# Low parts of later weights made in one buffer on GpSimd's queue, with an accumulating DMA

## The chip, the cores and the metric

The kernel runs on one core of one Trainium2 chip. The core has a matrix engine (TensorE, "PE" in the profile; "PEld" is its weight load), a vector engine (VectorE, "DVE"), a scalar engine (ScalarE, "ACT"), GpSimd ("POOL") and a queue engine that issues DMAs (SyncE, "SP"). ACT and POOL can issue DMAs too, in the order of their own queues. Each engine takes its instructions strictly in order: one that has to wait holds what stands behind it. The metric is the device time of one execution in microseconds, the median of several runs.

## What is computed

One decoder block over 1024 positions of width 1024, all in float32. A normed and modulated input `h` goes through one wide projection; two branches use its parts (stick-breaking attention, and a pooling over windows), gates mix them, and one more projection goes back to the residual stream:

```python
h = rms_norm(x, norm_gain) * (1.0 + scale) + shift
q, k, v, z_a, u, z_b, m_a, m_b = jnp.split(h @ w_in, offs, axis=-1)
p_a = (stick_breaking_attention(q, k, v) * silu(z_a)) @ w_branch_a
p_b = (multiscale_causal_pool(u, pool_w, pool_scale) * silu(z_b)) @ w_branch_b
merged = sigmoid(m_a) * p_a + sigmoid(m_b) * p_b
out = rms_norm(x + gate * (merged @ w_out), final_gain)
```

## The kernel before

The matrix engine is fed with `fp32r`, a rounded float32. To keep the accuracy of float32, each operand is split into a high part (the value, rounded to `fp32r`) and a low part (the value less its high part), and a product is made of three: high by high, high by low, low by high (`mm3`). So every weight tile of 128 x 1024 needs its low part somewhere.

The program runs through these stages, named by the tiles that the profile shows:

- `wm`, `ua`, `u`: the pooling maps are folded into weights, `h` is made, and the branch `u` is projected (its second half of the sequence, eight column tiles, in the loop that follows `load_wv` in the pool `vp`).
- `v`: the values, two halves of eight blocks each. Each block's result is split and stored to `v_d`.
- `wzb`: eight projections for the pooling branch's gate (`project(CZB + j, ...)`). Each loads its weights (`wzb_raw`), splits them on ACT and DVE, and its `silu` puts the result into `gb`. In the same loop, SP loads `w_gate` (`wg`), and DVE reduces it to the block's output gate.
- `p1` to `p7`: the product with `w_branch_b`, in seven half-size products of sums and differences (a Strassen scheme). Each has two halves; `a_op` splits the weights' side and `b_op` the other, on ACT and DVE. `load_a` (line 653) loads the weights' blocks on SP. For `p5`, each half needs three loads and adds them up on DVE.
- `p` in the attention stage: 40 projections with tiles `w` (queries, keys, gates), threaded by hand between the attention's own matmuls. Then `pa` and `o`, the two output projections.

The last 40 weight tiles are in the list `tiles`. The first eight (`PLAIN`) are split when they are loaded: high part on ACT, low part on GpSimd (`load_parts`, `split`, line 123) but for one on DVE. For the other 32, the low part is made ahead, during the `u`, `v`, `wzb` and `p1` to `p7` stages, and stored to the DRAM tensor `wl_d`; the attention stage loads it from there, beside the weights. `make_lo` (lines 147 to 165) does this: SP loads a tile into `lraw` (three buffers), ACT rounds it into `lhi` (one buffer), DVE subtracts in place, and SP stores the result. The tuples `LO_V`, `LO_ZB` and `LO_PB` say how many tiles are begun at each step of a stage: 8 in the `u` loop and 10 with `v` (in the pool `vp`), then 4 with `wzb` and 10 with the products (in the pool `pb`). `lraw` in `pb` also serves `wg` and, once, `gjunk`.

GpSimd's other work stands at both ends: small powers for the norm (line 260), and from the attention stage on the splits of the first weight tiles (line 123), the clearing of `kl` (line 790), two masks for each block of logits (`affine_select`, line 936) and a product at the end of each unit.

The order of each queue is made by the framework's planner from a simulation of the program, except for operations that `order` or `keep_in_program_order` pins: those of the first stage, and in the attention stage the matmuls and a few others. A pool's memory is used again by the pool opened after it is closed, and a tile there waits for the tiles whose place it takes. So the planner sets the place of `make_lo`'s steps in each queue, and the chip's waits then decide when they run.

Of the kernel before, what the change touches and what calls it, by code (L numbers as in the profile page):

```python
# [9 lines left out]
F32 = mybir.dt.float32  # L10
F32R = mybir.dt.float32r
AF = mybir.ActivationFunctionType
ALU = mybir.AluOpType
PSUM = bass.MemoryType.PSUM

P = 128
D = 1024
# [20 lines left out]

MASKED = 4
LO_V = (1, 0, 1, 1, 0, 1, 1, 0)  # L40
LO_ZB = (0, 1, 0, 1, 0, 1, 0, 1)
LO_PB = (1, 2, 1, 2, 1, 2, 1)

DIFFS = {1: 0, 4: 1, 7: 2, 10: 3}
HD = 64
# [12 lines left out]
def block_kernel(ctx, tc, a, out):  # L58
    nc = tc.nc
    v, act, gp = nc.vector, nc.scalar, nc.gpsimd  # L60

    def pool(name, **kw):
        return tc.tile_pool(name=name, bufs=1, reuse_waits="tile", **kw)
# [14 lines left out]
    def any_bank(name):  # L78
        return bank(next(turns), name)
# [8 lines left out]
    wl_d = dram.tile([5 * KB, P, D], F32, name="wl_d")  # L88
# [30 lines left out]
    def split(src, shape, pl, tag, bufs, hi_eng, lo_eng, name):  # L119
        hl = pl.tile([shape[0], 2] + list(shape[1:]), F32R, tag=tag, bufs=bufs, name=name)  # L120
        hi, lo = hl[:, 0], hl[:, 1]
        copy_to(hi_eng, hi, src)
        lo_eng.tensor_tensor(lo, src, hi.bitcast(F32), op=ALU.subtract)  # L123
        return hi, lo
# [15 lines left out]
    tiles = []  # L140
# [3 lines left out]
    tiles += gates  # L144
    early_lo = iter(range(PLAIN, len(tiles)))

    def make_lo(pl, n, bufs=3, later=False):

        rest = []
        for _ in range(n):  # L150
            i = next(early_lo)
            raw = pl.tile([P, D], F32, tag="lraw", bufs=bufs, name=f"l{i}_raw")
            hi = pl.tile([P, D], F32R, tag="lhi", bufs=1, name=f"l{i}_hi")
            nc.sync.dma_start(raw, a["w_in"][tiles[i]])

            def low(i=i, raw=raw, hi=hi):
                act.copy(hi, raw)  # L157
                v.tensor_sub(raw.bitcast(F32R), raw, hi.bitcast(F32))  # L158
                nc.sync.dma_start(wl_d[i], raw)

            if later:
                rest.append(low)
            else:
                low()
        return rest

    def load_parts(i, name):
        if i < PLAIN:
# [8 lines left out]
    def mm3(ps, whl, mhl, kbs, mov, first=True, last=True):  # L177
        (wh, wl), (mh, ml) = whl, mhl
        n = len(kbs)
        for i, kb in enumerate(kbs):  # L180
            for j, (w, m) in enumerate(((wh, mh), (wh, ml), (wl, mh))):
                mm(
                    ps, w[:, kb], mov(m, kb),
                    start=first and i == 0 and j == 0, stop=last and i == n - 1 and j == 2,
                )
# [4 lines left out]
    def hmov(sh):  # L190
        return lambda m, kb: m[:, kb, sh * 512:sh * 512 + 512]
# [25 lines left out]
    with pool("init") as init:  # L217
# [101 lines left out]
        wg, maps, halves = {}, {}, {}  # L319
# [66 lines left out]
        hi, lo_ = (0,), (1,)  # L386
        some, rest = slice(0, P), slice(P, D)
# [72 lines left out]
        for kb in range(KB):  # L460
            todo = [(i, kb) for i in range(len(accs))]
# [120 lines left out]
    with pool("vp") as vp:  # L582
        def load_wv(hf, k2):
            raw = wts.tile([P, 2, 512], F32, tag="raw", bufs=2, name=f"wv{hf}_{k2}_raw")
            nc.sync.dma_start(raw.rearrange("p k c -> p (k c)"), a["w_v"][hf, k2])
            return split(raw, [P, 2, 512], vp, "wv", 6, act, v, f"wv{hf}_{k2}")

        wv = [[load_wv(0, k2) for k2 in range(4)]]
        for i in reversed(range(KB)):
            ps = any_bank(f"u{i}_1")  # L590
            mm3(ps, whl[i], h, range(KB), hmov(1))
            use[i](1, ps)
            make_lo(vp, 1)
        early.close()
        diffs = ExitStack()
        todo = []
        dif = diffs.enter_context(pool("dif", side="right"))
        vouts = ExitStack()
        vop = vouts.enter_context(pool("vop", side="right"))
        for hf in range(2):  # L600
            if hf == 0:
                wv.append([load_wv(1, k2) for k2 in range(4)])
            for sb in range(8):
                ss = slice(sb * P, (sb + 1) * P)
                ps = any_bank(f"v{sb}_{hf}")
                for kb in range(KB):
                    hh, hl = h_hi[:, kb, ss], h_lo[:, kb, ss]
                    wh, wl = (w[:, kb % 2] for w in wv[hf][kb // 2])
                    for n, (l, w) in enumerate(((hh, wh), (hh, wl), (hl, wh))):
                        mm(ps, l, w, start=kb == 0 and n == 0, stop=kb == KB - 1 and n == 2)  # L610

                vo = vop.tile([P, 8, 2, HD], F32R, tag="vo", bufs=3, name=f"vo{sb}_{hf}")
                pv = ps.rearrange("p (h d) -> p h d", d=HD)
                act.copy(vo[:, :, 0], pv)
                v.tensor_sub(vo[:, :, 1], pv, vo[:, :, 0].bitcast(F32))
                nc.sync.dma_start(
                    v_d[4 * hf:4 * hf + 4, :, sb].rearrange("n p c -> p n c"),
                    vo.rearrange("p (n h) i d -> p n (h i d)", h=2).bitcast(F32),
                )

                now, todo = todo, make_lo(vp, LO_V[sb], later=True)
                if 8 * hf + sb in DIFFS:
                    j = DIFFS[8 * hf + sb]
                    todo.append(lambda j=j, u=load_u(j): make_d(j, u))
                for f in now:
                    f()
        assert not todo
        vouts.close()
# [3 lines left out]
    pb = pbs.enter_context(pool("pb"))  # L632
# [29 lines left out]
    for j in range(KB):  # L662
        if j not in dhls:
            make_d(j, load_u(j))

        def silu(sh, ps):
            z = gb[:, j, sh * 512:sh * 512 + 512]
            act.activation(z, ps, AF.Sigmoid)
            v.tensor_mul(z, ps, z)
            v.scalar_tensor_tensor(z, dhls[j][:, sh * 512:sh * 512 + 512], psc_v[:, j:j + 1], z, ALU.mult, ALU.mult)  # L670

        project(CZB + j, f"wzb{j}", silu, act, v)
        if j < 4:
            v.tensor_sub(t1[:, j], gb[:, j, 512:], gb[:, j, :512])
        else:
            v.tensor_sub(t2[:, j - 4], gb[:, j, 512:], t1[:, j - 4])
            v.tensor_sub(gb[:, j - 4, 512:], gb[:, j, 512:], gb[:, j - 4, 512:])
        make_lo(pb, LO_ZB[j])
        if j == 0:
            nc.sync.dma_start(sg, a["c_row"].broadcast_to([P, D]))  # L680
            gjunk = pb.tile([P, D], F32, tag="lraw", bufs=3, name="gjunk")
            act.activation(gjunk, sg, AF.Sigmoid)
            v.tensor_mul(sg, sg, gjunk)
        wg = pb.tile([P, D], F32, tag="lraw", bufs=3, name=f"wg{j}")
        nc.sync.dma_start(wg, a["w_gate"][j])
        v.scalar_tensor_tensor(wg, wg, 1.0, sg, ALU.mult, ALU.mult, accum_out=gate[:, j:j + 1])
        del dhls[j]
# [62 lines left out]
    for n, (name, a_of, b_of) in enumerate(products):  # L750
        c = {"p5": "b", "p3": "b", "p2": "c"}.get(name, "a")
        if c not in chain:
            chain[c] = [bank((tb if c == "b" else ta)[j], f"{name}_{j}") for j in range(4)]
        ps = chain[c]
        for q in range(2):
            wl_, ml_ = a_op(a_of(q), f"{name}a{q}"), b_op(b_of(q), f"{name}b{q}")
            for j in range(4):
                for e in range(2):
                    for i, (w, m) in enumerate(((0, 0), (0, 1), (1, 0))):
                        mm(  # L760
                            ps[j], wl_[:, w, e, j * P:(j + 1) * P], ml_[:, m, e],
                            start=name in ("p1", "p5", "p2") and (q, e, i) == (0, 0, 0), stop=(q, e, i) == (1, 1, 2),
                                skip_group_check=True,
                        )
        for j in range(4):
            if name == "p1":
                keep["s1", j] = copied("s1", 4, j, ps[j])
            elif name == "p6":
                keep["s2", j] = copied("s2", 4, j, ps[j])
            elif name == "p7":  # L770
                out_b(j + 4, 1, added(copied("s3", 2, j, ps[j]), chain["b"][j]))
            elif name == "p4":
                out_b(j + 4, 0, copied("s4", 2, j, ps[j]))
            elif name == "p3":
                out_b(j, 1, added(keep["s2", j], ps[j]))
            elif name == "p2":
                out_b(j, 0, added(keep["s1", j], ps[j]))
        make_lo(pb, LO_PB[n])
    pbs.close()


# [295 lines left out]
    with pool("fin") as fin:  # L1077
# [14 lines left out]
        for sh in range(2):  # L1092
            sl = slice(sh * 512, sh * 512 + 512)
            ms = []
            for j in range(KB):
# [9 lines left out]
                n = 0  # L1105
# [12 lines left out]
            for i in range(4):  # L1118
                sb = 4 * sh + i
# [7 lines left out]
                for c_, cl in enumerate(pieces):  # L1127
                    w_ = cl.stop - cl.start
                    ps = bank(("z", "tr")[c_ % 2], f"o{sb}_{c_}")[:, :w_]
                    n = 0  # L1130
# [85 lines left out]
```

## Time and profile before

| | |
|---|---|
| median of three runs | 1215.5 us (1214.86 to 1216.26) |
| the profiled execution | 1219.61 us, of which the span is 1217.9 us |
| mean granted clock of TensorE | 0.995 of full speed |

The profile is of one execution. Its page gives the busy time of each engine, the span in 40 slices with a digit of busy share for each, the groups of instructions by line, and the DMA queues. In rows of the order of time, the first two numbers are the start and the duration in us, then come engine, line, operation, output and inputs, the shape and the count; what stands in brackets is the idle time of the engine before it and what ended that. Rows of waits give the total in us, how often, and the longest. Rows of windows give the length and then for each engine the busy time, with the number of instructions.

### The profile page before, as it was taken

To read this page: it belongs to the slowest core of one execution; us is meant where nothing else is said; L and a number is where in the kernel's file an instruction comes from. 1 tells how busy PE (TensorE), PEld (TensorE's weight loads), DVE (VectorE), ACT (ScalarE), POOL (GpSimd) and SP (SyncE) were. 2 spreads that over 40 slices of the span, in tenths; PEclk is the share of its full clock that TensorE was granted. 3 is DMA by queue.
4 is the path that set the end of the run, shared out by engine and by line. 5 is a ranking of instruction groups with operands and counts; after the bars stand their busy time and mean duration, and the time that the engine had idled before them with its cause. 6 is when DMAs were issued, how large, how long until landed. Compare 5 with 4: busy or idle time off the path is not lost.

```text
span 1217.9 us, 16134 instructions
## 1 busy us (share of the span) xinstructions
PE 1194.0 (98%) x5698; PEld 995.8 (82%) x5698; DVE 796.7 (65%) x1088; ACT 549.9 (45%) x1020; POOL 167.9 (14%) x352
## 2 busy tenths in 40 slices
PE   8999999999699999999999999999999999999997
PEld 7888888887488888888888888888888888888886
DVE  5754591686675186777768678687777753795643
ACT  5564331332453255655656555555655653232211
POOL 1000000000000333222222221222221210000001
PEclk9999999999899999999999999999999999999999
DMA  9649994767735732343534325353353335985622
GB/s 350 259 168 360 308 380 169 231 221 166 271 138 178 224 92 70 107 135 104 162 116 138 101 95 164 110 155 99 110 143 100 96 123 173 352 273 168 208 72 84
DMA packets 85699, 212.39 MB, mean 174 GB/s; under 512 B 10609, under 2 KB 24049, under 8 KB 83442
## 3 DMA queue, kind: packets, MB, share of 16 engines
q1 hardware_dynamic: 77410, 196.47, 49.8%
q10 hardware_dynamic: 8208, 14.88, 3.3%
q8 instruction: 45, 0.74, 0.3%
q14 instruction: 36, 0.29, 0.1%
HBM read 144.20 MB, written 50.34 MB: 160 GB/s over the span
## 4 chain that ended last, share of the span: by engine, by line
PE 82%; DMA 7%; DVE 5%; issue 4%; ACT 1%; POOL 0%; SPq 0%; POOLq 0%; ACTq 0%; DVEq 0%
PE p L108 38%; PE v L108 7%; PE o L108 6%; PE z L108 6%; PE av L108 5%; PE wt L108 5%; PE pa L108 5%; PE u L108 4%; DMA wl_d<-l_raw 3%; PE ua L108 3%; DMA l_raw<-in_w_in 1%; PE wm L108 1%; DMA m<-sb_d 1%; PE wzb L108 1%; DMA kh<-kh 1%
## 5 line engine op out<-in xcount | busy, mean ns | idle before, releaser
L108 PE MATMUL p<-hT,w 128*128 128x512 f32 x1920 | 480.1, 391 | 0.6 <-ACT m_sg L203 0.6
L108 PEld LDWEIGHTS p<-hT,w 128*128 128x128 f32 x1920 | 355.2, 188 | 74.8 <-ACT m_sg L203 1.0
L938 DVE TENSOR_TENSOR_SCAN om<-om 128x512 f32<-128x512 f32 (+7 forms) x128 | 175.7, 1373 | 124.7 <-ACT om L931 69.1
L931 ACT ACTIVATE om<-z 128x512 f32<-128x512 f32 (+2 forms) x192 | 94.5, 492 | 156.4 <-PE z L108 133.9
L957 ACT CAST wt<-wt 128x512 fp32r<-128x512 f32 (+1 forms) x160 | 88.2, 551 | 48.2 <-PE wt L108 47.9
L958 DVE TENSOR_TENSOR wt<-wt,wt 128x512 fp32r<-128x512 f32 (+1 forms) x160 | 99.2, 620 | 16.2 <-ACT wt L957 15.6
L108 PE MATMUL av<-wt,vv 128*128 128x512 f32 x320 | 106.4, 414 | 0.0
L936 POOL TENSOR_SCALAR_AFFINE_SELECT om<-om 128x128 f32<-128x128 f32 x128 | 56.4, 441 | 346.9 <-ACT om L931 287.5
L108 DVE TENSOR_TENSOR be<-be,om 128x511 f32<-128x511 f32 (+7 forms) x128 | 95.1, 748 | 1.1 <-POOL be L936 0.7
L932 ACT ACTIVATE be<-z 128x512 f32<-128x512 f32 (+2 forms) x192 | 94.1, 490 | 0.0
L108 PE MATMUL pa<-ga,wa 128*128 128x512 f32 x384 | 89.9, 390 | 0.7 <-DVE s L1110 0.6
L108 PE MATMUL o<-wo,mhl 128*128 128x512 f32 (+1 forms) x408 | 89.6, 377 | 0.0
L108 PE MATMUL wzb<-hT,wzb 128*128 128x512 f32 x384 | 87.6, 390 | 2.0 <-DVE wzb L123 2.0
L108 PE MATMUL wt<-ident,be 128*128 128x128 f32 x576 | 89.4, 273 | 0.0
L108 PE MATMUL v<-wv,hT 128*128 128x512 f32 x384 | 87.2, 389 | 0.0
L108 PEld LDWEIGHTS wzb<-hT,wzb 128*128 128x128 f32 x384 | 71.9, 188 | 17.5 <-DVE wzb L123 2.5
L108 PEld LDWEIGHTS pa<-ga,wa 128*128 128x128 f32 x384 | 71.9, 188 | 16.4 <-issue 1.0
L108 PEld LDWEIGHTS o<-wo,mhl 128*128 128x128 f32 x408 | 73.5, 188 | 14.1
L108 PEld LDWEIGHTS v<-wv,hT 128*128 128x128 f32 x384 | 72.1, 188 | 14.9
L108 PEld LDWEIGHTS wt<-ident,be 128*128 128x128 f32 x576 | 70.2, 141 | 11.6
L157 ACT CAST l_hi<-l_raw 128x1024 fp32r<-128x1024 f32 x32 | 33.6, 1051 | 72.6 <-DMA l_raw<-in_w_in 54.8
L158 DVE TENSOR_TENSOR l_raw<-l_raw,l_hi 128x1024 fp32r<-128x1024 f32 x32 | 39.1, 1222 | 41.7 <-ACT l_hi L157 41.6
(175 smaller groups left out, 1481.8 us busy)
## 6 DMA issues: line engine op xcount, KB each, us to landing
w_raw<-in_w_in SPq DMA_DIRECT2D x40, 512.0 KB, 4.6
l_raw<-in_w_in SPq DMA_DIRECT2D x32, 512.0 KB, 4.9
wl_d<-l_raw SPq DMA_DIRECT2D x32, 512.0 KB, 5.9
w<-wl_d SPq DMA_DIRECT2D x32, 512.0 KB, 4.0
v_d<-vo SPq DMA_DIRECT2D x16, 512.0 KB, 5.2
vv<-v_d SPq DMA_DIRECT2D x8, 1024.0 KB, 5.3
wa_raw<-in_w_branch_a SPq DMA_DIRECT2D x16, 512.0 KB, 4.8
wa<-in_w_mod SPq DMA_DIRECT2D x7, 1024.0 KB, 6.3
```

What stands on the lines that cost most here:

```text
L108: ins = op(*args, **kw)
L157: act.copy(hi, raw)
L158: v.tensor_sub(raw.bitcast(F32R), raw, hi.bitcast(F32))
L931: act.activation(om[:, b0:b0 + n], zp[:, :n], AF.Sigmoid, scale=-0.125)
L932: act.activation(be[:, b0:b0 + n], zp[:, :n], AF.Sigmoid, scale=0.125)
L936: gp.affine_select(out=tl[:, :P], in_=tl[:, :P], pattern=[[1, P]], compare_op=ALU.is_gt, fill=fill, base=0, channel_multiplier=-1)
L938: v.tensor_tensor_scan(om[:, :W], om[:, :W], om[:, :W], 1.0, ALU.mult, ALU.min)
L957: act.copy(wt[:, 0, :off], pt[:, :off])
L958: v.tensor_sub(wt[:, 1, :off], pt[:, :off], wt[:, 0, :off].bitcast(F32))
```

## The change

`make_lo` no longer uses SP, ACT and DVE. GpSimd's queue loads the tile into one buffer `lo`; GpSimd reads it and writes the negative of its value, rounded to `fp32r`, over it; a DMA of the same queue loads the tile from DRAM again and adds it to what the buffer holds, which leaves the value less its high part; and that queue stores it to `wl_d`. The buffer `lhi` is gone, the `later` form too, so in the `v` loop the steps are no longer written behind the next block. `lraw` has four buffers in `vp` and three in `pb`. `wg` and `gjunk` get one buffer of their own. Two more tiles are begun with `wzb` and two fewer with the products: 8, 10, 6 and 8.

```diff
-LO_ZB = (0, 1, 0, 1, 0, 1, 0, 1)
-LO_PB = (1, 2, 1, 2, 1, 2, 1)
+LO_ZB = (0, 1, 1, 1, 0, 1, 1, 1)
+LO_PB = (1, 1, 1, 1, 1, 2, 1)
...
-    def make_lo(pl, n, bufs=3, later=False):
-
-        rest = []
+    def make_lo(pl, n, bufs=4):
+
         for _ in range(n):
             i = next(early_lo)
-            raw = pl.tile([P, D], F32, tag="lraw", bufs=bufs, name=f"l{i}_raw")
-            hi = pl.tile([P, D], F32R, tag="lhi", bufs=1, name=f"l{i}_hi")
-            nc.sync.dma_start(raw, a["w_in"][tiles[i]])
-
-            def low(i=i, raw=raw, hi=hi):
-                act.copy(hi, raw)
-                v.tensor_sub(raw.bitcast(F32R), raw, hi.bitcast(F32))
-                nc.sync.dma_start(wl_d[i], raw)
-
-            if later:
-                rest.append(low)
-            else:
-                low()
-        return rest
+            src = a["w_in"][tiles[i]]
+            lo = pl.tile([P, D], F32, tag="lraw", bufs=bufs, name=f"l{i}_raw")
+            gp.dma_start(lo, src)
+            gp.tensor_scalar(lo.bitcast(F32R), lo, -1.0, 0.0, op0=ALU.mult, op1=ALU.add)
+            gp.dma_start(lo, src, accum_op=ALU.add)
+            gp.dma_start(wl_d[i], lo)
...
-                now, todo = todo, make_lo(vp, LO_V[sb], later=True)
+                now, todo = todo, []
+                make_lo(vp, LO_V[sb])
...
-        make_lo(pb, LO_ZB[j])
+        make_lo(pb, LO_ZB[j], 3)
...
-            gjunk = pb.tile([P, D], F32, tag="lraw", bufs=3, name="gjunk")
+            gjunk = pb.tile([P, D], F32, tag="wg", bufs=1, name="gjunk")
...
-        wg = pb.tile([P, D], F32, tag="lraw", bufs=3, name=f"wg{j}")
+        wg = pb.tile([P, D], F32, tag="wg", bufs=1, name=f"wg{j}")
...
-        make_lo(pb, LO_PB[n])
+        make_lo(pb, LO_PB[n], 3)
```

## The prediction

> **What bounds it now.** I read the page from the top: the busy table says which engine sets the time, the row of slices says where that engine isn't busy.
>
> ```profile
> span 1217.9 us, 16134 instructions
> PE 1194.0 (98%) x5698; PEld 995.8 (82%) x5698; DVE 796.7 (65%) x1088; ACT 549.9 (45%) x1020; POOL 167.9 (14%) x352
> PE   8999999999699999999999999999999999999997
> PEclk9999999999899999999999999999999999999999
> ```
>
> TensorE is busy 98% of the span; no change that leaves the matmuls alone can win more than 1217.9 - 1194.0 = 23.9 us and what a lowered clock adds. Only one slice in the middle shows less than a 9, the eleventh (304 to 335 us), and the granted clock dips in the same slice. The order of time of PE shows this stage, the end of the `wzb` projections and the first products:
>
> ```profile
> 215.48 76.87 PE L108 MATMUL wzb<-hT,wzb 128*128 128x512 f32 x338
> 294.38 10.73 PE L108 MATMUL wzb<-hT,wzb 128*128 128x512 f32 x46 [2.04 <-DVE wzb L123]
> 310.05 1.22 PE L108 MATMUL p<-p1b,p1a 128*128 128x512 f32 x2 [4.94 <-ACT p1a L658]
> 311.61 6.71 PE L108 MATMUL p<-p1b,p1a 128*128 128x512 f32 x22 [0.34 <-DVE p1a L659]
> 321.88 7.22 PE L108 MATMUL p<-p1b,p1a 128*128 128x512 f32 x24 [3.56 <-ACT p1a L658]
> 330.85 11.28 PE L108 MATMUL p<-p5b,p5a 128*128 128x512 f32 x48 [1.74 <-ACT p5a L658]
> ```
>
> The brackets are idle time: 2.04 + 4.94 + 0.34 + 3.56 + 1.74 = 12.6 us. And the matmuls beside the gaps are slow. Undisturbed, one takes 76.87 / 338 = 0.227 us. At that rate the 142 of the five later rows would take 32.3 us; they took 10.73 + 1.22 + 6.71 + 7.22 + 11.28 = 37.2. That is 4.9 us more, and the windows of the stage show a lower granted clock there (columns: PE, PEld, DVE, ACT, POOL busy, then clock, DMA share, GB/s):
>
> ```profile
> 300.00:310.00 10.00, 5.11 (x23) 3.91 (x21) 3.29 (x4) 3.52 (x4) 0.00 (x0) 0.89 0.84 286
> 310.00:320.00 10.00, 7.93 (x24) 5.61 (x24) 7.32 (x9) 3.24 (x4) 0.00 (x0) 0.77 0.92 338
> 320.00:330.00 10.00, 7.22 (x24) 5.50 (x24) 7.28 (x8) 4.20 (x7) 0.00 (x0) 0.83 0.62 236
> 340.00:400.00 60.00, 60.00 (x264) 49.21 (x263) 35.08 (x36) 25.55 (x31) 4.18 (x2) 1.00 0.46 154
> ```
>
> So the stage holds 12.6 + 4.9 = 17.5 us, and from 340 on PE is full at full clock. Who made the gaps? ACT's order of time, and SP's waits between 205 and 345 us:
>
> ```profile
> 301.52 1.05 ACT L157 CAST l_hi<-l_raw 128x1024 fp32r<-128x1024 f32 x1 [5.66 <-DMA l_raw<-in_w_in]
> 307.52 1.04 ACT L157 CAST l_hi<-l_raw 128x1024 fp32r<-128x1024 f32 x1 [4.96 <-DMA l_raw<-in_w_in]
> 308.48 0.59 ACT L668 ACTIVATE gb<-wzb 128x512 f32<-128x512 f32 x1
> 308.96 1.03 ACT L658 CAST p1a<-a 128x1024 fp32r<-128x1024 f32 x1
> 319.36 1.04 ACT L157 CAST l_hi<-l_raw 128x1024 fp32r<-128x1024 f32 x1 [2.26 <-DMA l_raw<-in_w_in]
> 320.80 1.03 ACT L658 CAST p1a<-a 128x1024 fp32r<-128x1024 f32 x1
> ...
> SPq L154 <- DMA wl_d<-l_raw: 42.8, 8, 12.0
> SPq L159 <- DVE l_raw L158: 13.4, 8, 4.3
> ```
>
> ACT stood at a low part's cast until its load landed, and `p1a`'s cast, ready to go, stood behind it in the queue: twice, just ahead of the two `p1` gaps. The load was late because SP held it until an earlier low part's store had freed the buffer. So 8.5 us of the gaps (4.94 + 3.56), and the clock with them, hang on low parts that these products don't use.
>
> **The change, part by part.** It takes out, for each of 32 tiles, one cast, one subtraction and two SP issues:
>
> ```profile
> L157 ACT CAST l_hi<-l_raw 128x1024 fp32r<-128x1024 f32 x32 | 33.6, 1051 | 72.6 <-DMA l_raw<-in_w_in 54.8
> L158 DVE TENSOR_TENSOR l_raw<-l_raw,l_hi 128x1024 fp32r<-128x1024 f32 x32 | 39.1, 1222 | 41.7 <-ACT l_hi L157 41.6
> l_raw<-in_w_in SPq DMA_DIRECT2D x32, 512.0 KB, 4.9
> wl_d<-l_raw SPq DMA_DIRECT2D x32, 512.0 KB, 5.9
> L154 SPq DMA_DIRECT2D l_raw<-in_w_in x32: 327/333/742, 69.5 to 314.0; - x32
> ```
>
> That is 33.6 us of ACT and 39.1 of DVE, worth nothing where PE is full, and the blocking at the stage above, worth up to 17.5 us. It adds POOL work: 32 negations, and 96 DMA issues of which 32 accumulate.
>
> The negation reads one 128x1024 tile. No row has it; POOL's nearest are a memset of 64x1024 (949 ns) and a subtraction of two such tiles (2396 ns, below). I take 1.7 us, halfway. The accumulating DMA isn't in the trace either. At least it is a load, 4.9 us; it also has to read and rewrite the tile, so at most a load and a store, 4.9 + 5.9 = 10.8. I take 7.9, the middle, as no row is nearer. One tile's way is then load 4.9, negation 1.7, accumulation 7.9, store 5.9: 20.4 us. The three POOL issues take at least SP's 0.33 us each and, bounded by POOL's longest instruction, at most 2.4; with some 1 us each and the crowded stage below I take 27 us. Its ends: with the shortest rows, 4.9 + 0.95 + 4.9 + 5.9 = 17; with every DMA as slow as the slowest of these tiles now (13.1 us), 3 x 13.1 + 2.4 = 42.
>
> The Trainium skill's page "DMA: Bandwidth & Descriptors", section on the anatomy of a DMA from GpSimd, fits such a transfer as 2.0 us + bytes / 436 GB/s: an estimate of 3.2 us for 512 KB, and a chain of 3 x 3.2 + 1.7 = 11 us, below my low end; no row here shows POOL's queue.
>
> 18 tiles go through four buffers (eight in the `u` loop, ten with `v`), 14 through three. With C the way of one tile that is C x (18/4 + 14/3) = 9.2 C, from 69.5 us on: at 27 us it ends near 318 us, about where the old pipeline ended; at 17 near 225; at 42 near 455. What is queued behind it on POOL:
>
> ```profile
> 66.78 0.55 POOL L260 TENSOR_TENSOR st<-st,mhalf 128x1 f32<-128x1 f32 x1 [0.69 <-ACT junk L108]
> 392.73 2.41 POOL L123 TENSOR_TENSOR w<-w_raw,w 128x1024 fp32r<-128x1024 f32 x1 [325.40 <-ACT w L128]
> ...
> 423.87 0.29 POOL L936 TENSOR_SCALAR_AFFINE_SELECT om<-om 128x128 f32<-128x128 f32 x1 [0.97 <-ACT om L931]
> ```
>
> POOL does nothing between 67 and 393 us, so the added work is hidden as long as C stays under (393 - 69.5) / 9.2 = 35 us. The reused buffer is waited for on POOL alone now. SP keeps the `wg` loads, in one buffer instead of a share of three; a wait of SP there holds `wzb_raw` behind it. One such load and its use, 4.7 us and 1.2, fit in the 10.9 us of a projection, so I cost it at nothing.
>
> DMA is the resource that gets fuller:
>
> ```profile
> 145.00:155.00 10.00, 10.00 (x46) 8.29 (x45) 6.75 (x7) 3.02 (x4) 0.00 (x0) 1.00 1.01 335
> 165.00:175.00 10.00, 10.00 (x46) 8.29 (x45) 10.00 (x14) 4.71 (x6) 0.00 (x0) 1.00 1.04 386
> 195.00:205.00 10.00, 10.00 (x46) 8.29 (x45) 0.92 (x2) 0.79 (x2) 0.00 (x0) 1.00 0.30 105
> q1 hardware_dynamic: 24800, 60.83, 72.2%
> a<-in_w_branch_b SPq DMA_DIRECT2D x10, 512.0 KB, 5.0
> ```
>
> Between 80 and 330 us SP's queue moved 60.83 MB in 72.2% of 250 us, so 0.52 MB takes 1.55 us of all 16 engines. The 32 accumulations add 50 us at one such share and 99 at two, to a stage with 70 us free. The stage around 150 us is full already, but PE doesn't wait in it, and 195 to 205 is nearly empty. The likelier loss is at `p5`, where one half (5.4 us of matmuls) needs three loads of 512 KB and the low parts may still be under way. Even now DVE waited there for such a load:
>
> ```profile
> 328.49 1.23 DVE L706 TENSOR_TENSOR a<-a,a 128x1024 f32<-128x1024 f32 x1 [1.97 <-DMA a<-in_w_branch_b]
> ```
>
> I let the 1.74 us gap at `p5` stand and grow by another 1.97. The sum, against the profiled run of 1219.6 us (1.7 more than its span): 1219.6 - 17.5 + 3.7 = 1205.8. The median of the timed runs is 1215.5, 4.1 below that run, so 1201.7 us.
>
> **The rivals.** *The transfers take it back.* The low parts run on past 330 at half the engines' time, the loads of `branch_b` come late for `p1`, `p5` and `p7`, and half of the 17.5 us stays or returns: 1215.5 - 8.7 = 1206.8, up to 1213. For it speaks the three-load half of `p5`; against it that after 340 the share of DMA is 0.46. If all the gaps return in that way, it is no change, 1213 to 1218.
>
> *DVE isn't relieved.* POOL's masks vary fourfold at one shape:
>
> ```profile
> 424.36 0.29 POOL L936 TENSOR_SCALAR_AFFINE_SELECT be<-be 128x128 f32<-128x128 f32 x1 [0.19 <-ACT be L932]
> 433.54 1.23 POOL L936 TENSOR_SCALAR_AFFINE_SELECT be<-be 128x128 f32<-128x128 f32 x1
> ```
>
> If they slow when DVE is at work, DVE can be held as well: 14 negations of 1.7 us are 24 us in the stage from 216 on, against 14 x 1.22 = 17 freed. The 2.04 us gap stays and each of `p1`'s two subtractions may come 1.7 late: 1201.7 + 5.4 = 1207. The Trainium skill, "SBUF — State Buffer", section "Who interferes with whom", has this as a rule: a DVE instruction with two SBUF inputs and a GpSimd one that reads SBUF shut each other out for a whole instruction. By that rule these two masks agree, though the trace doesn't say who came first.
>
> *POOL is late for attention.* This is the slower side. If C is above 35 us, or the planner's order lets a tile's accumulation wait in front of the next loads so that fewer than four are under way, POOL comes late to the split at 393 and PE to the first attention projection. Each us of C beyond 35 costs 9.2: at 40 us it is 46, 1198 + 46 = 1244. For it speaks that nothing shows what accumulating costs; against it that C would have to come out a third above mine.
>
> *It doesn't do what it says.* The planner orders each queue itself, so taking the casts off ACT need not bring `p1a` forward: if the `a` load is still issued as late as now, its landing keeps `p1` late. ACT's cast at 308.96 has no bracket, so the load was there; this would end within the first rival's range.
>
> **How the numbers follow.** Forecast, most gaps gone (1197 to 1206): 0.47. Half taken back, 1206 to 1213, by transfers 0.14 or by DVE 0.09. No change: 0.12. POOL late, or another queue made late by more than the gain: 0.18. A difference of 0.2% (2.4 us) is about what a measurement of this kernel can tell from none; faster gets 0.47 + 0.14 + 0.09 = 0.70. The floor is 1215.5 - 17.5 = 1198; a little below for run scatter, the range begins at 1196. At 1219 some 0.15 of the slower case lies above, and 0.03 under 1196.
>
> **What would show it.** Right: no bracket above 1 us on PE between 290 and 330, clock 1.00 there, ACT's casts of `p1a` before 303 us, wait of SP on stores gone, POOL's last low store issued before 393. Wrong: POOL's first split of `w` later than 393 with PE waiting for it; PE waits on `a` loads; accumulations landing after more than 11 us.

## The result, and the profile after

The changed kernel took 1234.06 us (median of four runs, 1231.97 to 1235.78) beside 1215.88 us for the kernel before: the ratio is 1.0145, with a 95% interval of 1.0122 to 1.0169. It is slower by 1.5%, where 1201.7 us, 1.1% faster, was forecast. The profiled execution took 1231.97 us, its span 1229.9.

From the page of the changed kernel: the busy table, the slices of PE and of the DMA engines, and the queues (packets, MB, share of 16 engines over the span).

```profile
span 1229.9 us, 16071 instructions
PE 1197.4 (97%) x5698; PEld 997.2 (81%) x5698; DVE 772.6 (63%) x1056; ACT 517.7 (42%) x988; POOL 271.3 (22%) x480
PE   8999989999789999999999999999999999999997
DMA  9749999999965724263433535334263225975622
q1 hardware_dynamic: 68194, 162.92, 40.3%
q0 software_dynamic: 13824, 50.34, 14.1%
```

ACT is relieved as forecast, from 549.9 to 517.7 us. DVE goes from 796.7 to 772.6 us, 24.1 less where subtractions of 39.1 us were taken out: its other instructions took 15.0 us longer. The gap in the eleventh slice didn't go, the twelfth now has one too, and so has the sixth, in the `v` stage, where there had been none. The DMA row shows a 9 in every slice from the fourth to the eleventh. The order of time of PE in the changed kernel, all its rows with an idle bracket above 3 us:

```profile
178.74 0.79 PE L108 MATMUL v<-wv,hT 128*128 128x512 f32 x1 [4.47 <-ACT wv L128]
187.19 40.06 PE L108 MATMUL v<-wv,hT 128*128 128x512 f32 x169 [3.02 <-DVE wv L123]
...
330.33 5.47 PE L108 MATMUL p<-p1b,p1a 128*128 128x512 f32 x16 [6.30 <-DVE p1a L651]
346.62 3.18 PE L108 MATMUL p<-p5b,p5a 128*128 128x512 f32 x8 [4.42 <-ACT p5a L650]
```

Why did `wv` come late, a weight whose loads were all issued before 118 us? ACT's order of time in the changed kernel:

```profile
152.10 0.59 ACT L605 CAST vo<-v 128x512 fp32r<-128x512 f32 x1 [7.13 <-DMA v_d<-vo]
165.95 0.59 ACT L605 CAST vo<-v 128x512 fp32r<-128x512 f32 x1 [9.32 <-DMA v_d<-vo]
177.15 0.58 ACT L605 CAST vo<-v 128x512 fp32r<-128x512 f32 x1 [10.62 <-DMA v_d<-vo]
177.63 1.99 ACT L128 CAST wv<-wv_raw 128x1024 fp32r<-128x1024 f32 x2
```

ACT stood at the cast of `v`'s results until one of the three `vo` buffers came free, and the cast of `wv` stood behind it. It is the same picture as before the change, a cast that is held and another one held behind it, but now a store is what is late. That made the gap of 4.47 us. The one of 3.02 us has another late transfer behind it, a load of `u`. DVE's order of time:

```profile
183.92 1.24 DVE L562 TENSOR_TENSOR win<-u 128x1039 f32<-128x1039 f32 x1 [3.98 <-DMA u<-u_d]
185.08 2.06 DVE L123 TENSOR_TENSOR wv<-wv_raw,wv 128x1024 fp32r<-128x1024 f32 x1
```

DVE stood at `win` until the load landed, and the subtraction of `wv`, whose cast was long done, stood behind it. The gap at `p1` is of the same kind, with a load of `wg`:

```profile
327.25 1.23 DVE L678 SCALAR_TENSOR_TENSOR wg<-wg,sg 128x1024 f32<-128x1024 f32 x1 [4.16 <-DMA wg<-in_w_gate]
329.06 1.22 DVE L651 TENSOR_TENSOR p1a<-a,p1a 128x1024 fp32r<-128x1024 f32 x1
```

The issues of DMAs give the median time to landing; first the kernel before, then the changed one:

```profile
v_d<-vo SPq DMA_DIRECT2D x16, 512.0 KB, 5.2
u<-u_d SPq DMA_DIRECT2D x8, 512.0 KB, 5.9
wzb_raw<-in_w_in SPq DMA_DIRECT2D x8, 512.0 KB, 5.4
```

```profile
v_d<-vo SPq DMA_DIRECT2D x16, 512.0 KB, 15.2
u<-u_d SPq DMA_DIRECT2D x8, 512.0 KB, 12.4
wzb_raw<-in_w_in SPq DMA_DIRECT2D x8, 512.0 KB, 11.3
```

Nothing about these transfers was changed; they land two to three times as late. The windows from 128 to 330 us (PE, PEld, DVE, ACT, POOL busy; clock; DMA share; GB/s), before and after, show with whom they shared the engines:

```profile
128.00:330.00 202.00, 190.23 (x819) 155.33 (x817) 131.58 (x172) 61.14 (x77) 0.00 (x0) 0.97 0.75 249
```

```profile
128.00:330.00 202.00, 186.33 (x801) 151.80 (x799) 109.61 (x140) 35.58 (x50) 79.01 (x100) 0.97 1.02 316
```

The DMA share went from 0.75 to 1.02 for 200 us: the engines had work nearly all the time. (The share adds up the times of packets, and those that overlap count twice, so it can pass 1.)

The gap at `p5` is not of this kind. At 330.8 us, as soon as the last `wg` is used, SP issues the store of the finished gate to `g_d` (line 681): 4 KB, written as 1024 packets of 4 bytes. The loads that `p5` waits for are issued beside it and after it, from 330.3 to 335.8 us. The windows before, behind and after these packets:

```profile
323.00:329.00 6.00, 1.03 (x5) 0.53 (x3) 1.84 (x4) 0.29 (x1) 1.60 (x3) 0.82 1.03 412
335.00:341.00 6.00, 5.47 (x24) 4.04 (x23) 5.56 (x4) 2.46 (x4) 2.88 (x3) 1.00 0.36 38
341.00:347.00 6.00, 1.58 (x8) 0.99 (x7) 2.36 (x2) 2.52 (x3) 0.00 (x0) 1.00 0.95 206
```

For six us the engines moved 38 GB/s, with loads waiting and a share of 0.36, and the last of these loads took 14.8 us to land. Other runs show the same lull behind this store (33 GB/s between 276 and 282 us in the kernel before, 20 between 313 and 319 in e5 below). In the kernel before the store was issued at 271.2 us, in the `wzb` stage, and PE was busy throughout the lull. In the changed kernel the late `wg` loads pushed it onto the loads for `p5`. No run moves this store alone, so what it costs is read from the traces and not shown by an experiment.

On POOL itself nothing was late for attention, the last two rows of its order of time that matter:

```profile
350.86 0.55 POOL L156 DMA_DIRECT2D wl_d<-l_raw  x1 [2.87 <-DMA l_raw<-in_w_in]
405.90 2.41 POOL L123 TENSOR_TENSOR w<-w_raw,w 128x1024 fp32r<-128x1024 f32 x1 [54.49 <-ACT w L128]
```

The last low part was stored at 351 us, and POOL then waited 54 us for ACT.

### The profile page after: what moved, and what is told of

The parts are those of the page before. It is cut to its first block, busy times and chain, and to the rows that moved or that the text cites. A ratio compares the mean times of both kernels' runs of the same rounds, so it can differ in the third digit from the quotient of the medians.

```text
span 1229.9 us, 16071 instructions
## 1 busy us (share of the span) xinstructions
PE 1197.4 (97%) x5698; PEld 997.2 (81%) x5698; DVE 772.6 (63%) x1056; ACT 517.7 (42%) x988; POOL 271.3 (22%) x480
## 3 DMA queue, kind: packets, MB, share of 16 engines
q0 software_dynamic: 13824, 50.34, 14.1%
## 4 chain that ended last, share of the span: by engine, by line
PE 78%; DMA 13%; DVE 5%; issue 2%; ACT 1%; SPq 0%; POOL 0%; POOLq 0%; ACTq 0%; DVEq 0%
PE p L108 39%; PE o L108 6%; PE av L108 5%; PE z L108 5%; PE wt L108 5%; PE pa L108 5%; DMA u<-u_d 4%; PE wzb L108 4%; PE v L108 3%; PE ua L108 3%; DMA u_d<-u_sg 3%; DMA wg<-in_w_gate 2%; PE wm L108 1%; DMA a11s<-in_w_branch_b 1%; PE u L108 1%
## 5 line engine op out<-in xcount | busy, mean ns | idle before, releaser
L930 DVE TENSOR_TENSOR_SCAN om<-om 128x512 f32<-128x512 f32 (+7 forms) x128 | 175.5, 1371 | 124.8 <-ACT om L923 69.5
L108 PE MATMUL v<-wv,hT 128*128 128x512 f32 x384 | 91.4, 400 | 8.0 <-ACT wv L128 4.5
L108 PEld LDWEIGHTS o<-wo,mhl 128*128 128x128 f32 x408 | 73.5, 188 | 14.1
L108 PE MATMUL z<-kl,q 128*128 128x512 f32 (+2 forms) x192 | 65.5, 341 | 0.0
L108 PE MATMUL z<-kh,q 128*128 128x512 f32 (+2 forms) x192 | 64.0, 333 | 0.4 <-DMA q<-qlo 0.4
## 6 DMA issues: line engine op xcount, KB each, us to landing
v_d<-vo SPq DMA_DIRECT2D x16, 512.0 KB, 15.2
```

What stands on the lines that cost most here:

```text
L108: ins = op(*args, **kw)
L930: v.tensor_tensor_scan(om[:, :W], om[:, :W], om[:, :W], 1.0, ALU.mult, ALU.min)
```

## The experiments

All times are medians; the ratio is to the kernel before in the same group of runs (1215.9 to 1217.1 us), with its 95% interval. e1, e5, e6 and e12 leave the accumulation out for all or half of the tiles, so what they store to `wl_d` is not the low part; they are there for their time alone.

| run | us | ratio | interval |
|---|---|---|---|
| changed kernel | 1234.1 | 1.0145 | 1.0122 to 1.0169 |
| e1: without the accumulating DMA | 1201.3 | 0.9874 | 0.9858 to 0.9891 |
| e2: changed, two buffers | 1242.4 | 1.0213 | 1.0198 to 1.0229 |
| e3: subtraction on GpSimd | 1226.9 | 1.0091 | 1.0076 to 1.0106 |
| e4: before, with a second store | 1215.3 | 0.9991 | 0.9982 to 1.0000 |
| e5: a plain load for the accumulation | 1215.3 | 1.0003 | 0.9985 to 1.0020 |
| e6: every second tile accumulates | 1210.7 | 0.9951 | 0.9933 to 0.9969 |
| e7: before, GpSimd's queue | 1214.7 | 0.9993 | 0.9975 to 1.0011 |
| e8: changed, two buffers for `wg` | 1232.5 | 1.0127 | 1.0091 to 1.0163 |
| e9: e7 with all low parts early | 1217.2 | 1.0001 | 0.9983 to 1.0018 |
| e10: before, accumulating from `wzb` on | 1210.8 | 0.9961 | 0.9942 to 0.9980 |
| e11: before, all low parts early | 1209.4 | 0.9946 | 0.9929 to 0.9963 |
| e12: four plain transfers per tile | 1231.9 | 1.0124 | 1.0068 to 1.0181 |

### e1: the accumulating DMA left out

```diff
             gp.tensor_scalar(lo.bitcast(F32R), lo, -1.0, 0.0, op0=ALU.mult, op1=ALU.add)
-            gp.dma_start(lo, src, accum_op=ALU.add)
             gp.dma_start(wl_d[i], lo)
```

> The changed kernel without the accumulating DMA (what is stored to wl_d is then the negative high part). GpSimd's queue still loads, negates and stores, but moves a third less: 33.6 MB in place of 50.3. Theory A, the 16.8 MB that accumulating adds fill the DMA engines: their share between 128 and 330 us falls from 1.02 to about 0.8, v_d's stores land within 8 us again (15.2 in the changed kernel, 5.2 before), PE's 8 us of gaps in the v stage go, 1198 to 1208 us. Theory B, it is the queue: a second queue that always has work takes half or more of the engines' time whatever it carries: v_d's stores still land after 12 us or more, gaps in v stay, 1218 to 1234 us. Theory C, the planner's other order of SP and ACT alone: no change to the changed kernel, 1230 to 1236.

1201.3 us, 32.8 below the changed kernel. Its window, its share of GpSimd's queue and the stores to `v_d`:

```profile
128.00:330.00 202.00, 202.00 (x892) 166.95 (x891) 128.14 (x159) 45.35 (x62) 51.28 (x67) 1.00 0.73 257
```

```profile
q0 software_dynamic: 9216, 33.56, 7.4%
v_d<-vo SPq DMA_DIRECT2D x16, 512.0 KB, 7.3
```

PE is busy for all of the 202 us at full clock: theory A. So the queue, the planner's new order and POOL's negations cost nothing that PE sees in this run; all of the loss, and more, comes with this one DMA. PE was busy too between 128 and 216 us, where the share was 1.00 even here. The run can't tell whether a third transfer or the adding is to blame. It gives a price: 64 plain transfers took 7.4% of 1199.3 us, 1.39 us of all 16 engines each. In the changed kernel the queue took 14.1% of 1229.9 us, 173.4; less the 88.7 of the 64 plain ones, one accumulation took 84.7 / 32 = 2.65 us, 1.9 times a plain transfer. This is an estimate: the same transfers are charged other times in other runs. With the 1.49 us of a plain one in e5 (below) the same subtraction leaves 2.4 us, and in e2, with the changed kernel's transfers, GpSimd's queue took 15.2% of 1238.4 us, which gives 3.1.

### e5 and e6: what of it is the adding, and how the loss grows

```diff
-            gp.dma_start(lo, src, accum_op=ALU.add)
+            gp.dma_start(lo, src)
```

> The changed kernel with the accumulating DMA replaced by a plain load of the same tile into the same buffer, at the same place in GpSimd's queue (so wl_d gets the weights themselves). Waits, issues and the 50.3 MB of that queue stay; only the adding is gone. Theory D, the adding itself is dear: by the shares of GpSimd's queue an accumulation took 2.65 us of all 16 engines (14.1% of 1229.9 us less 64 plain transfers of 1.39 us each, 32 of them) where a plain transfer takes 1.39; then this run has 32 x 1.26 = 40 us less DMA time and comes to 1201 to 1212 us. Theory B, a third transfer per tile on a queue of its own, whatever it does: 1222 to 1236.

1215.3 us, between the two ranges: theory D's size was wrong. A plain third transfer costs 14.0 us beside e1, the adding another 18.8. The one gap above 1 us that PE has in e5's profile between 128 and 400 us, 9.46 us at `p5`, ends with a load of `a` that was issued at 312.0 us, just behind the store to `g_d` (308.9 us), and took 13.9 us to land. So most of this price is paid where a late transfer meets that store.

```diff
-            gp.dma_start(lo, src, accum_op=ALU.add)
+            if i % 2:
+                gp.dma_start(lo, src, accum_op=ALU.add)
```

> The changed kernel with the accumulating DMA for every second tile only, 16 of 32 (the others store the negative high part). If the loss goes with the number of accumulations: half of the 32.8 us between 1201.3 and 1234.1, so 1214 to 1221. If it begins only where the engines run full for longer than the loads' slack (a threshold): 1201 to 1209.

1210.7 us, again between: half of the accumulations cost 9.4 of the 32.8 us, where half the loss would be 16.4. The loss grows faster than the load. The largest gap in e6's profile is 6.23 us in `v`, where DVE stands at `win` for a load of `u`, with `wv`'s subtractions behind it.

### e12: four plain transfers in place of three, one of them adding

```diff
-            gp.dma_start(lo, src, accum_op=ALU.add)
+            gp.dma_start(lo, src)
             gp.dma_start(wl_d[i], lo)
+            gp.dma_start(ws_d[i], lo)
```

> The run with a plain second load in place of the accumulation, and a second store of each low part, to a DRAM tensor that nobody reads, behind the first on GpSimd's queue: four plain transfers per tile, none of them adding. By the share of GpSimd's queue, four plain transfers of 1.38 us each take 32 x 4 x 1.38 = 177 us of all engines; the changed kernel's three, one of them adding, took 173; three plain ones 143. Theory E, what an accumulation costs is its engine time and nothing else: 1228 to 1240, v_d's stores landing after 13 us or more. Theory F, adding holds something else (its landing in a tile's chain, memory, the buffer): four plain transfers cost as three or a little more, 1214 to 1224.

1231.9 us, theory E. Its queue's share and the stores to `v_d`:

```profile
q0 software_dynamic: 18432, 67.12, 14.3%
v_d<-vo SPq DMA_DIRECT2D x16, 512.0 KB, 17.8
```

14.3% of 1227.4 us is 175.5, as much as in the changed kernel, and without any adding the time is the same within its scatter (1223.9 to 1237.9). With this the five runs of one program, which differ in one line or two, stand in a table by the engine time of GpSimd's queue (its share of the span, times the span):

| run | GpSimd's queue, us of all engines | DMA share, 128 to 330 us | time, us | over e1, us |
|---|---|---|---|---|
| e1 | 88.7 | 0.73 | 1201.3 | 0 |
| e6 | 132.1 | 0.91 | 1210.7 | 9.4 |
| e5 | 143.0 | 0.96 | 1215.3 | 14.0 |
| changed | 173.4 | 1.02 | 1234.1 | 32.8 |
| e12 | 175.5 | 0.98 | 1231.9 | 30.7 |

The first 43 us cost 9.4; the 30 from e5 to the changed kernel cost 18.8. What the transfers do makes no difference to the time that these runs can tell, how long they hold the engines does. Where the gaps then appear is not fixed: the changed kernel has them in `v`, at `p1` and at `p5`; e12 has 3.00 us in `wzb`, 8.51 at `p5` and 4.21 at the start of attention. In e12 the stores to `v_d` land even later than in the changed kernel, and ACT stands at `vo` for 58.9 us in all beside 53.5. Yet PE has no gap in `v`, because the two casts of `wv` came at 171.0 us in place of 177.6, which was just in time. So a late landing costs nothing until it passes the moment at which PE needs what stands behind it, and the equal times of the two kernels are made of different gaps.

### e4: the same bytes where there is room

```diff
                 nc.sync.dma_start(wl_d[i], raw)
+                gp.dma_start(ws_d[i], raw)
```

> The kernel before with each low part stored a second time, from GpSimd's queue, into a DRAM tensor that nobody reads: 16.8 MB more, and nothing else moved. Theory A (bytes): 32 x 1.55 = 50 us more of all engines' time, the share between 128 and 330 us rises from 0.75 to about 0.95, 1220 to 1232. Theory B (queue): GpSimd's queue has one short transfer per tile and is mostly empty, so it takes little from SP's: 1215 to 1220.

1215.3 us, no slower: 3.8% of 1213.2 us, 46 us of engine time on GpSimd's queue, cost nothing in the kernel before, though the share between 128 and 330 us rose from 0.75 to 0.89. Theory A's price for bytes as such was wrong. The last low part is stored at 349 us in place of 322, and the median time is no longer for that. In the profile the largest gaps are now at `p5` (2.39 and 4.61 us) and no longer at `p1`.

### e2: fewer under way at a time

```diff
-    def make_lo(pl, n, bufs=4):
+    def make_lo(pl, n, bufs=2):
...
-        make_lo(pb, LO_ZB[j], 3)
+        make_lo(pb, LO_ZB[j], 2)
...
-        make_lo(pb, LO_PB[n], 3)
+        make_lo(pb, LO_PB[n], 2)
```

> The changed kernel with two buffers for the low parts instead of four and three, so at most two of GpSimd's transfers are under way. Theory A (too much to move in the time): the same bytes spread over longer, the low parts end near 400 us instead of 351, the gaps in v shrink from 8 to 2 us or none, and part of them returns at p1 to p7 or at attention's start: 1220 to 1236. Theory B (the queue's share): one transfer under way is as good as four, the v gaps stay near 8 us and the low parts end at most 30 us later: 1232 to 1245.

1242.4 us, worse than the 1220 to 1236 of theory A, and as slow as theory B, but with A's signs: `v_d`'s stores land after 6.0 us, one gap of 2.30 us is left in `v`, and the last low part is stored at 398 us. The waits were moved to the later stages (order of time of PE):

```profile
268.29 12.08 PE L108 MATMUL wzb<-hT,wzb 128*128 128x512 f32 x46 [6.40 <-DVE wzb L123]
...
347.05 10.39 PE L108 MATMUL p<-p5b,p5a 128*128 128x512 f32 x32 [15.80 <-ACT p5a L650]
```

Two things stand behind these gaps, and neither is the price of a transfer. The tiles of the pool `pb` take the place of `vp`'s: SP waited 16.9 us, until 248 us, for the store of a low part before it could go on to the loads of `gbias` and `sg`, and the chain of work that ended last goes through these. And the gap at `p5` again has the store to `g_d` just ahead of it (324.6 us); between 327 and 335 us the engines moved 28 GB/s, and a load of `a` took 18 us to land. So e2 doesn't tell what fewer transfers at a time would be worth without these two.

### e3: no accumulation, the subtraction on GpSimd

```diff
+            hi = pl.tile([P, D], F32R, tag="lhi", bufs=1, name=f"l{i}_hi")
-            gp.tensor_scalar(lo.bitcast(F32R), lo, -1.0, 0.0, op0=ALU.mult, op1=ALU.add)
-            gp.dma_start(lo, src, accum_op=ALU.add)
+            gp.tensor_scalar(hi, lo, 1.0, 0.0, op0=ALU.mult, op1=ALU.add)
+            gp.tensor_tensor(lo.bitcast(F32R), lo, hi.bitcast(F32), op=ALU.subtract)
```

> The low part made on GpSimd without accumulating: load, high part into a second buffer, subtraction, store, all on GpSimd (buffers 3 + 1 in vp, 2 + 1 in pb). The bytes are those of the kernel before, the queue that of the changed one. Theory A: 1198 to 1208, DMA share about 0.8. Theory B: 1218 to 1234, v_d's stores still late. If GpSimd's two-input reads hold DVE, DVE's busy time rises above the changed kernel's 772.6 us by over 20 and PE's waits name DVE: 1208 to 1218.

1226.9 us, and neither for theory A's reason nor for B's: `v_d`'s stores land after 5.8 us, but PE has a gap of 15.08 us in `v`, and DVE is named. It is the third case, beyond its range. DVE's groups between 80 and 345 us, from e1 and from e3 (busy us, mean ns, idle before):

```profile
L123 DVE TENSOR_TENSOR wv<-wv_raw,wv 128x1024 fp32r<-128x1024 f32 x8 | 10.6, 1331 | 15.9 <-ACT wv L128 10.6 <-DMA u_d<-u_sg 5.3
L605 DVE TENSOR_TENSOR vo<-v,vo 128x512 fp32r<-128x512 f32 x16 | 11.0, 688 | 57.2 <-ACT vo L604 57.2
```

```profile
L123 DVE TENSOR_TENSOR wv<-wv_raw,wv 128x1024 fp32r<-128x1024 f32 x8 | 17.1, 2171 | 9.3 <-ACT wv L128 9.3
L607 DVE TENSOR_TENSOR vo<-v,vo 128x512 fp32r<-128x512 f32 x16 | 10.9, 684 | 27.4 <-ACT vo L606 27.4
```

The same subtraction takes 2.17 us in place of 1.33 when POOL subtracts beside it, while the one that reads its first input from PSUM stays at 0.68. DVE's busy time is 808.3 us, 39.6 above e1's 768.7 and 35.7 above the changed kernel's. The Trainium skill ("SBUF — State Buffer", section "Who interferes with whom") says that a DVE instruction with two inputs in SBUF and a GpSimd instruction that reads SBUF shut each other out; the two rows agree.

### e7, e9 and e11: what the queue is worth

e7 is the kernel before with the loads and stores of the low parts on GpSimd's queue:

```diff
-            nc.sync.dma_start(raw, a["w_in"][tiles[i]])
+            gp.dma_start(raw, a["w_in"][tiles[i]])
...
-                nc.sync.dma_start(wl_d[i], raw)
+                gp.dma_start(wl_d[i], raw)
```

> The kernel before with only the low parts' loads and stores moved from SP's queue to GpSimd's; ACT's cast and DVE's subtraction stay. If SP's waits on the low parts' stores were what held ACT and PE: no bracket above 2 us on PE between 290 and 335 us, 1200 to 1207. If ACT still stands at the casts because a buffer comes free late, whoever issues the load: gaps at p1 stay, 1208 to 1217.

1214.7 us, no change that can be told, in the second range. ACT still stands at the casts, and `p1a`'s cast behind them (ACT's order of time, and the wait of POOL's queue for its buffers between 205 and 345 us):

```profile
307.50 1.05 ACT L157 CAST l_hi<-l_raw 128x1024 fp32r<-128x1024 f32 x1 [5.07 <-DMA l_raw<-in_w_in]
313.56 1.04 ACT L157 CAST l_hi<-l_raw 128x1024 fp32r<-128x1024 f32 x1 [5.01 <-DMA l_raw<-in_w_in]
314.50 0.59 ACT L668 ACTIVATE gb<-wzb 128x512 f32<-128x512 f32 x1
314.99 1.03 ACT L658 CAST p1a<-a 128x1024 fp32r<-128x1024 f32 x1
...
POOL l_raw L154 <- DMA wl_d<-l_raw: 37.0, 9, 12.1
```

SP's queue was not the reason: the buffers come free late, whoever issues the load. POOL waits for the stores as SP did, 37.0 us in place of 42.8. The Trainium skill says so in general ("DMA: Bandwidth & Descriptors", section "Issuing engines are not separate DMA queues"): issuing from another engine saves only that engine's issue time. This run agrees. e11 leaves the queues and moves the casts away from the products:

```diff
-LO_V = (1, 0, 1, 1, 0, 1, 1, 0)
-LO_ZB = (0, 1, 0, 1, 0, 1, 0, 1)
-LO_PB = (1, 2, 1, 2, 1, 2, 1)
+LO_V = (2, 2, 2, 1, 2, 1, 2, 0)
+LO_ZB = (0, 0, 0, 0, 0, 0, 0, 0)
+LO_PB = (0, 0, 0, 0, 0, 0, 0)
```

> The kernel before with all 32 low parts begun in the u and v stages and their transfers left on SP's queue. Beside the run with the same placement on GpSimd's queue it tells what the queue is worth: if SP's waits on stores hold wzb's and wv's loads, 1208 to 1220 and slower than that run by over 4 us; if the queue is worth nothing, within 3 us of it.

> The kernel before with the low parts' transfers on GpSimd's queue and all 32 begun in the u and v stages (LO_V adds up to 24 in place of 10, LO_ZB and LO_PB to nothing), still cast on ACT and subtracted on DVE. If what held p1 was ACT standing at low parts' casts among the products, no bracket is left between 290 and 335 us: 1198 to 1205. If the v stage can't carry 14 more on its engines, PE gets gaps there that cost 5 to 15 us: 1206 to 1216.

e11 took 1209.4 us, the lowest median of the versions that make the low parts in full (e10's 1210.8 can't be told from it), ahead of both kernels. Its one gap above 1 us between 128 and 400 us is at `p5` (order of time of PE):

```profile
319.05 13.39 PE L108 MATMUL p<-p5b,p5a 128*128 128x512 f32 x48 [5.92 <-ACT p5a L658]
```

e9, the same placement with GpSimd's queue, took 1217.2 us, 7.8 more: there the queue of its own is a loss. Neither run came out as expected: e9 was to have no gap after 290 us, or gaps in `v`, and e11 was to be slower than e9 or equal. In e9 PE had gaps of 2.74 and 1.70 us in `wzb` and 7.66 at `p5`, with DVE and ACT named; why the queue makes them is not settled.

### e8 and e10: two parts of the change

e8 gives `wg` and `gjunk` two buffers (and `s3` and `s4` one, to make room):

```diff
-        wg = pb.tile([P, D], F32, tag="wg", bufs=1, name=f"wg{j}")
+        wg = pb.tile([P, D], F32, tag="wg", bufs=2, name=f"wg{j}")
```

> The changed kernel with two buffers for wg in place of one (the outputs s3 and s4 of the products get one each, to make room). If the one buffer, in which eight loads and their uses follow each other on SP and DVE, is what holds p1a's subtraction (6.3 us of gap on PE, DVE at wg loads ahead of it), that gap goes and the time falls by 5 to 8 us, to 1226 to 1229. If it is the late landing of transfers alone, the gap stays at some 6 us: 1232 to 1236.

1232.5 us, from 1225.7 to 1235.3: the median is in the second range, the profiled run (1225.7, the fastest) beside the first, so the time decides nothing. In its profile the 6.3 us gap at `p1` is gone, those in `v` stay (4.52 and 3.91), and gaps of 2.2 and 2.1 at `p5` and 1.1 to 1.2 at `p4` stand, two of the latter behind the copies of the outputs, whose buffers were halved. So the single buffer did make that gap as far as one profile tells, but what its removal wins can't be told from this run.

e10 makes the 18 low parts of the `u` and `v` stages as before, and only the 14 later ones by accumulation:

```diff
-        make_lo(pb, LO_ZB[j])
+        make_lo_acc(pb, LO_ZB[j])
...
-        make_lo(pb, LO_PB[n])
+        make_lo_acc(pb, LO_PB[n])
```

> The 18 low parts of the u and v stages made as before, the 14 of the wzb and product stages as in the changed kernel, by accumulating DMA on GpSimd's queue. If accumulations hurt only where the engines are full already (the v stage), no gap in v, and those ahead of p1 go with ACT's casts: 1202 to 1210. If 14 of them are enough to make wg's and branch_b's loads late: gaps at p1 and p5 of 8 us or more, 1211 to 1222.

1210.8 us, 0.8 above the first range and with its signs: no gap in `v`, none at `p1`, one of 4.46 at `p5`, behind a load of `a` that was issued just behind the store to `g_d` and took 15.7 us to land. With ACT's casts gone from the later stages, the kernel with these fourteen accumulations is 5.5 us faster than before, at a share of 0.97 between 128 and 330 us.

## Why the prediction was wrong

- **What bounds the kernel, and the gain.** Right: 17.5 us of gaps and slow clock hung on ACT's and DVE's low parts. e1, the change less its accumulation, has none of them and took 1201.3 us. That 1201.7 was forecast is partly luck: the sum held 3.7 us of gaps that e1 doesn't have, and without them it gives 1198.
- **Who held ACT.** Half right. The prediction had SP hold the load back until a store had freed the buffer. The buffer was the reason, SP's queue was not: e7 took SP out and ACT waited as long (5.07 and 5.01 us, beside 5.66 and 4.96). So the gain comes with the casts leaving ACT and DVE.
- **The way of one tile.** Right in the main. C was put at 27 us; the loads into the first of the four buffers were issued at 116.7, 143.9, 172.7 and 202.2 us, 27 to 30 apart, and those into the first of three from 230 us on 22 to 25 apart. The parts were off and cancelled in part: the negation took a median of 1.3 us for 1.7, the accumulation landed after 9.4 for 7.9, the store after 8.1 for 5.9. The last store was issued at 351 us and not near 318, since POOL began its second load only at 90 us and stood from 208 to 230 between the two pools. POOL wasn't late for attention, so the first half of the slower case didn't come.
- **The step that failed: the price of fuller DMA engines.** The 32 accumulations were put at 50 to 99 us of all engines, in a stage with 70 free; they took 84.7 by e1's price. That was within the bounds and more than the room, which by the share of all queues (0.75 of 250 us) was 62 and not 70. But the sum charged only 1.97 us for it, at `p5`, because "PE doesn't wait" in the full stage around 150 us. That held only as long as what PE needed still landed in time. In the changed kernel the stores to `v_d` landed after 15.2 us in place of 5.2 and the loads of `u` after 12.4 in place of 5.9; ACT stood at `vo`, DVE at `win`, and PE got 8 us of gaps in `v`. The loads of `wg` came late for `p1` (6.30 us) and pushed the store to `g_d` onto the loads for `p5` (4.42 and 1.03 us). The size, beside e1, is 32.8 us where 1.97 stood.
- **The rivals.** "The transfers take it back" named the mechanism, but stopped at "no change", since it let the old gaps return and not new ones open in stages without any. The chances did hold what came, as the second half of one line, "another queue made late by more than the gain" (0.18 together with a late POOL), but no time was worked out for it. Of the signs of being wrong, PE's wait for `a` loads at `p5` came; accumulations landing after more than 11 us did not, as a median (9.4 us).
- **The wait for `wg`** was costed at nothing, with a load of 4.7 us; three of them in a row took 6 to 8 us each in the chain of work, ahead of `p1a`'s subtraction on DVE.
- **DVE not relieved:** in part. Of 39.1 us taken out, 24.1 came off DVE's busy time (796.7 to 772.6), and the gaps at `wv` and `p1a` name late loads, not POOL; with a subtraction on POOL (e3) it decides.

## What to carry to other kernels

Before moving work from an engine to a DMA, add up the engine time of all transfers in the stage, the new ones at their own price, and compare it with the room that is left: near a share of 1 the loss came through other transfers, those with few buffers, and grew faster than the load. The share alone is no verdict: at 0.89 e4 lost nothing, at 0.97 e10 still won 5.5 us. What decides is which transfers land late and what stands behind them in the queues of ACT and DVE. A stage in which DMA is full and the matrix engine doesn't wait, as `v` in e1, has slack in the landing of its transfers, not free bandwidth. As far as the traces tell, a small store of many tiny packets belongs in a stage where nobody waits for a load; no run tested that alone. Where a waiting cast holds others behind it, moving the cast in time (e11) was worth more than moving its DMAs to another queue (e7).

## What the runs showed of the hardware that wasn't expected

- One accumulating DMA of 512 KB into SBUF took some 2.65 us of all 16 engines by the estimate under e1 (2.4 to 3.1 by other runs), about twice a plain one (1.39 in e1, 1.49 in e5), and landed after a median of 9.4 us, where the plain load at its place in e5 landed after 6.8. POOL needed a median of 0.889 us to issue it, and 0.582 for the plain load in e5.
- Between 128 and 216 us GpSimd's queue had 69.5% of the engines' time in the changed kernel, SP's 33.7% (overlapping packets count twice); before, SP's queue, with the low parts in it, had 76.8%. The stores to `v_d`, on SP's queue, landed later by 10 us in the changed kernel, but by only 1.0 and 2.1 us in e7 and e1, which also have a queue on GpSimd. So a second queue alone doesn't explain it, and how the engines are shared between two queues is not settled here.
- A store of 4 KB in 1024 packets of 4 bytes (`g_d`) was followed by a lull of 6 us or more in which the engines moved 20 to 48 GB/s with loads waiting (the changed kernel, the kernel before, e2, e5 and e10), where they moved up to 412 GB/s otherwise.
